# TensorE's order in the gated-DeltaNet recurrence of a hybrid decoder step, written out by hand

## The chip, the core and the metric

The kernel runs on one core of a Trainium2 chip. The metric is the device time of one execution in microseconds (us); less is better. Engines are named as in the profile: PE (TensorE), PEld (its weight loads), DVE (VectorE), ACT (ScalarE), POOL (GpSimd) and SP (SyncE, which here issues most of the DMAs).

## What is computed

One inference step of a two-layer decoder for a prompt of 256 tokens and eight samples of one token each, 264 columns in all, in float32. Each sub-layer ends in a LayerNorm. Layer 0 holds half a feed-forward block, the mixer, cross-attention and a second half feed-forward; layer 1 holds a spatial gating block in the mixer's place. The change is in the mixer:

```
proj = h @ ab_w_in                                  # 1024 -> 3*512 (q,k,v) + 512 (z) + 8 + 2*512 (ga, gb)
q, k, v = split(silu(causal_conv4(qkv)))            # 4 heads of 128
q, k = l2_normalize(q) * 128**-0.5, l2_normalize(k)
beta, g = sigmoid(b), -exp(A_log) * softplus(a + dt)
o, S = gated_delta_rule(q, k, v, g, beta, S0)       # chunks: solve (I + M) sol = rhs, then a scan over chunks
o = rms_norm(o, dn_norm_g) * silu(z)
c = causal_conv31(ga * sigmoid(gb))                 # depthwise, 512 channels
c = silu(layer_norm(c + cc_conv_b))
y = concat([o, c]) @ ab_w_out
```

## The kernel before

Activations lie transposed, channels on the 128 partitions and the 264 tokens along the row. Every projection is cut into units of 128 output channels. A unit is 24 matmuls, called products here: 8 slices of the 1024 inputs, each three times, since operands are split into a high and a low part of a shorter float format (`Unit.products`, line 659; high by high, low by high, high by low). The weights come in blocks of 256 output channels (1 MB, `load_w`, line 192, tile `raw`, three buffers); for each unit ACT writes the high part (`whi`, line 224) and DVE the low part (`wlo`, line 217), four buffers of each. Products add up in one of four PSUM tiles `mm`; all small matmuls use four others, `ax`.

The mixer (`mixer`, line 828) runs in this order in the program: projections of q, k and v with their four-tap convolution (`ev_qkv`), squares for the norms (1038, 1041), gates and decay matrices DT for two chunks of 128 tokens (1061 to 1110), the inverse of a triangular matrix in five levels of blocks up to 32 (1226 to 1251), two merges of blocks to 64 and to 128, the chunk scan (1304 to 1330), and beside it a generator `sample_step` that does the eight samples' recurrence in pieces (`next(steps, None)`). Behind it stand `glu` (the gates ga and gb; gb needs a Sigmoid on ACT), `taps` (the 31-tap convolution: the gated rows are stored to DRAM, read back shifted by 0 to 3 tokens, `cinx`, and 32 small matmuls per 128 channels do four taps each, line 932), `zeta` (z), `conv_norm` (the LayerNorm behind the taps), four units of attention keys (`fill`), the output gating and `update` (new states of the samples). `attention` and `out_proj` follow.

Only some instructions are pinned to the order of the program (`pin`, line 143). For the rest a scheduler picks the order of each engine, and it pulls `glu`, `taps` and `zeta` forward between the recurrence's matmuls. `cinx` and its weights use the three `raw` buffers of the projections' weights. The lines that set this:

```
pin(PE.matmul(self.ps, lhsT=self.w[q // 2][:, k, :], rhs=self.rhs[q % 2][:, k, :], ...), pinned)      # a product
buf = wpool.tile([P, KT, 256], F32, tag="raw", name="cinx", bufs=3)                                   # the taps' input
```

Of the kernel before, what the change touches and what calls it, by code (L numbers as in the profile page):

```python
# [15 lines left out]
P = 128  # L16
# [19 lines left out]
def decoder_step_kernel(  # L36
# [235 lines left out]


    class Norm:
# [7 lines left out]
        def __init__(self, idx, scale, eps, units=None, on_pe=False, place=None):  # L282
# [5 lines left out]
            self.S = work.tile([P, T], F32, tag="lnS", name="lnS", bufs=1)  # L288
            self.Q = work.tile([P, T], F32, tag="lnQ", name="lnQ", bufs=1)
# [26 lines left out]
        def add(self, k, ps):  # L316
# [4 lines left out]
            if k == 1:  # L321
                s01 = work.tile([P, T], F32, tag="lns01", name="lns01", bufs=1)
# [8 lines left out]
                else:  # L331
                    ca = work.tile([P, T], F32, tag="lnca", name="lnca", bufs=1)
# [57 lines left out]
        def fixed(self, ps):  # L390

            w2 = work.tile([P, 2], F32, tag="fixw", name="fixw", bufs=4)
            A.copy(w2, ps[:, T:])
            t = work.tile([P, T], F32, tag="fix", name="fix", bufs=2)
            pin(V.scalar_tensor_tensor(out=t, in0=self.ndl, scalar=w2[:, 0:1], in1=ps[:, :T], op0=ALU.mult, op1=ALU.add), True)  # L395
            pin(V.tensor_tensor(out=t, in0=t, in1=self.r, op=ALU.mult), True)
            return t, w2[:, 1:2]

        def finish(self, kv, evac, at):
# [9 lines left out]
            self.ndl = work.tile([P, T], F32, tag="lnca", name="lndl", bufs=1)  # L409
# [418 lines left out]
    def mixer(nrm, fillers, mp):  # L828
# [3 lines left out]

        cp_ctx = tc.tile_pool(name="conv", bufs=1, reuse_waits="tile")
# [66 lines left out]
        gbt = {}  # L900

        def ev_gb(n, ps):
            gbt[n] = mp.tile([P, T], F32, tag="gb", name="gb", bufs=2)
            A.activation(out=gbt[n], in_=ps, func=AF.Sigmoid)
# [4 lines left out]
        def glu(n2):  # L909
            proj(ab_w_in, 2056 + 512 + 256 * n2, 2, rhs, lambda n, ps: ev_gb(2 * n2 + n, ps))  # L910
            proj(ab_w_in, 2056 + 256 * n2, 2, rhs, lambda n, ps: ev_ga(2 * n2 + n, ps))
            for n in range(2 * n2, 2 * n2 + 2):
                SP.dma_start(cin_d[n], cin[:, n, 0:30 + NP])

        def taps(n):

            W = NP + 28
            buf = wpool.tile([P, KT, 256], F32, tag="raw", name="cinx", bufs=3).rearrange("p k n -> p (k n)")
            xs = buf[:, :4 * W].rearrange("p (g t) -> p g t", g=4)
            w07 = buf[:, 4 * W:4 * W + 7 * P].rearrange("p (j g m) -> p j g m", j=7, g=4)  # L920
            w7 = mp.tile([P, 4, 32], F32, tag="cw", name="cw")
            G.memset(xs[96:128, :, W - 1:], 0.0)
            SP.dma_start(w07, cw_d[n][:, 0:7])
            SP.dma_start(w7, cw_d[n][:, 7])
            src = cin_d[n].rearrange("(g c) t -> c g t", c=32)
            for s in range(4):
                w = W - 1 if s == 3 else W
                SP.dma_start(xs[32 * s:32 * s + 32, :, :w], src[:, :, s:s + w])
            pv = mm_ps()
            for j in range(8):  # L930
                for g in range(4):
                    PE.matmul(pv[32 * g:32 * g + 32, :NP], lhsT=w07[:, j, g, :] if j < 7 else w7[:, g, :], rhs=xs[:, g, 4 * j:4 * j + NP], start=j == 0, stop=j == 7)  # L932
# [3 lines left out]
            V.tensor_scalar(out=o[:, NP:], in0=cs_[:, n, :], scalar1=par[:, n, R_CCB:R_CCB + 1], scalar2=None, op0=ALU.add)  # L936

# [59 lines left out]
        def ev_z(n, ps):  # L997
            A.activation(out=zs[:, n, :], in_=ps, func=AF.Silu)
            G.tensor_scalar(out=zs[:, n, :], in0=zs[:, n, :], scalar1=dng, scalar2=None, op0=ALU.mult)

        def zeta(h):
            proj(ab_w_in, 1536 + 256 * h, 2, rhs, lambda n, ps: ev_z(2 * h + n, ps))
# [26 lines left out]

        q, kk, v = qkv  # L1030

# [3 lines left out]
        for i, t in enumerate((kk, q)):  # L1035
            for c in range(2):
# [3 lines left out]
                for h in range(H):  # L1040
                    PE.matmul(pss[32 * h:32 * h + 32, m:m + P], lhsT=ones[1][:, 0:32], rhs=sq[:, h, :], start=True, stop=True)
        st = gp.tile([P, 512], F32, tag="Y", name="st", bufs=2)
        A.copy(st, pss)
        pss = ax_ps()
        for m in range(4):
            PE.transpose(pss[:, m * P:(m + 1) * P], st[:, m * P:(m + 1) * P], ident)
# [14 lines left out]
        PE.matmul(pc[:, 0:8], lhsT=tri, rhs=gv[:, 0:2, :], start=True, stop=True)  # L1061
# [7 lines left out]
        for c in range(2):  # L1069
            cs = TOK[c]  # L1070

            tg = gp.tile([P, H, P], F32, tag="tg", name="tg", bufs=2)
            for h in range(H):
                if 'AAAAAAAA'[4 * c + h] == 'A':
                    A.mul(tg[:, h, :], tri, gv[:, c, h:h + 1])
                else:
                    (V if 'AAAAAAAA'[4 * c + h] == 'V' else G).tensor_scalar(out=tg[:, h, :], in0=tri, scalar1=gv[:, c, h:h + 1], scalar2=None, op0=ALU.mult)
            pg = ax_ps()
            PE.matmul(pg, lhsT=ones[1], rhs=tg.rearrange("p h i -> p (h i)"), start=True, stop=True)
# [7 lines left out]
            for h in range(H):  # L1087
                A.activation(out=DT[c][:, h, :], in_=DT[c][:, h, :], func=AF.Exp, bias=ngc[:, c, h:h + 1])
            pk = ax_ps()
            for h in range(H):  # L1090
                PE.matmul(pk[:, h * P:(h + 1) * P], lhsT=kk[:, h, cs], rhs=kk[:, h, cs], start=True, stop=True)
            NT[c] = gp.tile([P, H, P], F32, tag=f"NT{c}", name="NT")
            for h in range(H):
                V.scalar_tensor_tensor(out=NT[c][:, h, :], in0=hd(pk)[:, h, :], scalar=br2[:, c, h:h + 1], in1=DT[c][:, h, :],
                                       op0=ALU.mult, op1=ALU.mult)
            pq = ax_ps()
            for h in range(H):
                PE.matmul(pq[:, h * P:(h + 1) * P], lhsT=kk[:, h, cs], rhs=q[:, h, cs], start=True, stop=True)
# [6 lines left out]

            pv = ax_ps()
            for h in range(H):
                PE.transpose(pv[:, h * P:(h + 1) * P], v[:, h, cs], ident)
# [11 lines left out]
        def sample_step():  # L1120
# [7 lines left out]
            PE.matmul(pkq[:, :64], lhsT=ones[1], rhs=kq2, start=True, stop=True)  # L1128
# [654 lines left out]
```

## Time and profile before

| what | us |
|---|---|
| three runs | 1391.05, 1386.64, 1386.5 (median 1386.64) |
| the profiled execution, its own time | 1388.67 |
| its span, first to last instruction | 1387.0 |
| PE busy | 1345.1 (97%) |
| DVE busy | 937.1 (68%) |
| ACT busy | 742.6 (54%) |
| POOL busy | 202.7 (15%) |

The table's times but the first row are of one profiled execution, and those of the engines add up what each was busy; they overlap. A busy PE is one that has matmuls under way, not one at its peak. The clock that the chip granted PE (PEclk; 1.00 is 2.4 GHz, 0.50 is 1.2 GHz) averages 0.983 over the span. The page also follows the chain of work that ended last back from the end: 71% of the span lie on PE, 44% of it on line 659, the products.

### The profile page before, as it was taken

The page shows a single profiled execution, that of the slowest core. Times are in us where ns is not written, and L with a number is a line of the kernel's source. Part 1 is how long each engine was busy: PE and PEld are TensorE (multiplying, and loading weights), DVE is VectorE, ACT ScalarE, POOL GpSimd, SP SyncE. Part 2 cuts the span into 40 slices and gives each one's busy share as a digit, 9 for nine tenths or more (in the row PEclk, how much of TensorE's full clock was granted, in tenths as well). Part 3 has the DMA queues.
Part 4 walks back from the last instruction along what each step waited for, and adds up shares of the span by engine and source line. Part 5 has one row for each costly group of instructions (what it writes and reads, how often), then busy time and mean ns, then how long its engine had stood idle before and what let it go on. Part 6 is the DMA issues. An engine that isn't in the chain of part 4 may idle for free.

```text
span 1387.0 us, 27352 instructions
## 1 busy us (share of the span) xinstructions
PE 1345.1 (97%) x10951; PEld 1272.8 (92%) x10951; DVE 937.1 (68%) x1911; ACT 742.6 (54%) x1362; POOL 202.7 (15%) x244
## 2 busy tenths in 40 slices
PE   8999999988989999999999999999999999999997
PEld 8999999866879978999999999999999868999996
DVE  5555668865658776975556865566988987855454
ACT  4455447774545544664445654445766635744432
POOL 3312410301111000111121011121112001011021
PEclk9999999999989999999999999999999999999998
DMA  7654766435659888455556655556548893555551
GB/s 261 215 165 161 240 196 178 140 110 145 185 184 313 286 276 263 149 176 182 184 177 195 215 171 181 180 175 193 186 143 275 284 304 119 188 189 183 185 175 37
DMA packets 270543, 269.27 MB, mean 194 GB/s; under 512 B 8243, under 2 KB 266291, under 8 KB 270400
## 3 DMA queue, kind: packets, MB, share of 16 engines
q1 hardware_dynamic: 257408, 260.97, 59.5%
q10 hardware_dynamic: 13008, 6.55, 1.8%
q8 instruction: 86, 1.41, 0.4%
q14 instruction: 41, 0.34, 0.1%
HBM read 252.81 MB, written 15.26 MB: 193 GB/s over the span
## 4 chain that ended last, share of the span: by engine, by line
PE 71%; DVE 5%; ACT 4%; DMA 2%; issue 1%; POOL 0%; POOLq 0%; ACTq 0%; DVEq 0%
PE mm L659 44%; PE mm L818 5%; PE mm L817 5%; PE mm L819 5%; PE mm L711 3%; PE ax L1686 1%; PE ax L1657 1%; DMA S_s<-in_state_dn_S_dram 1%; ACT whi L224 1%; PE ax L1636 1%; DVE wlo L217 1%; PE ax L1615 1%; DMA raw<-in_ab_w_in_dram 0%; PE mm L932 0%; ACT XT L1207 0%
## 5 line engine op out<-in xcount | busy, mean ns | idle before, releaser
L217 DVE TENSOR_TENSOR wlo<-raw,whi 128x1024 fp32r<-128x1024 f32 (+1 forms) x380 | 460.8, 1220 | 252.1 <-ACT whi L224 248.3
L224 ACT CAST whi<-raw 128x1024 fp32r<-128x1024 f32 (+1 forms) x380 | 389.3, 1031 | 418.9 <-PE mm L659 219.9
L659 PE MATMUL mm<-xhi,whi 128*128 128x264 f32 x1728 | 496.2, 288 | 5.3 <-ACT whi L224 5.2
L659 PE MATMUL mm<-xhi,wlo 128*128 128x264 f32 x1728 | 496.3, 288 | 3.3 <-DVE wlo L217 3.3
L659 PE MATMUL mm<-xlo,whi 128*128 128x264 f32 x1728 | 495.1, 287 | 0.2
L659 PEld LDWEIGHTS mm<-xhi,whi 128*128 128x128 f32 x1728 | 328.3, 190 | 10.2 <-ACT whi L224 6.7
L659 PEld LDWEIGHTS mm<-xhi,wlo 128*128 128x128 f32 x1728 | 327.0, 190 | 8.7 <-DVE wlo L217 4.2
L659 PEld LDWEIGHTS mm<-xlo,whi 128*128 128x128 f32 x1728 | 329.0, 190 | 2.9 <-issue 1.4
L817 PE MATMUL mm<-hh,whi 128*128 128x264 f32 x704 | 200.6, 285 | 0.0
L818 PE MATMUL mm<-hl,whi 128*128 128x264 f32 x704 | 200.1, 284 | 0.0
L819 PE MATMUL mm<-hh,wlo 128*128 128x264 f32 x704 | 199.8, 284 | 0.0
L817 PEld LDWEIGHTS mm<-hh,whi 128*128 128x128 f32 x704 | 132.6, 188 | 0.1
L819 PEld LDWEIGHTS mm<-hh,wlo 128*128 128x128 f32 x704 | 132.4, 188 | 0.0
L818 PEld LDWEIGHTS mm<-hl,whi 128*128 128x128 f32 x704 | 132.3, 188 | 0.1
L187 POOL TENSOR_TENSOR hl<-sg,hh 128x264 fp32r<-128x264 f32 x44 | 61.1, 1388 | 444.1 <-ACT hh L180 444.1
L659 PE MATMUL mm<-xpre,whi 128*128 128x266 f32 x640 | 117.3, 290 | 1.6 <-DVE fix L395 1.6
L659 PEld LDWEIGHTS mm<-xpre,whi 128*128 128x128 f32 x640 | 97.9, 189 | 2.8 <-ACT x L443 1.4
L659 PE MATMUL mm<-xpre,wlo 128*128 128x266 f32 x320 | 85.2, 288 | 0.0
L368 POOL TENSOR_TENSOR lnQ<-lnQ,lnsq 128x264 f32<-128x264 f32 x40 | 41.7, 1042 | 296.7 <-ACT lnsq L361 296.6
L765 DVE TENSOR_TENSOR sg<-mm,sg 128x264 f32<-128x264 f32 x76 | 32.9, 433 | 50.6 <-PE mm L659 50.0
L659 PEld LDWEIGHTS mm<-xpre,wlo 128*128 128x128 f32 x320 | 57.7, 189 | 0.1
L1620 DVE CUSTOM_DVE_ANT_0 junk<-cache,ax 128x256 f32<-128x256 f32 x128 | 47.3, 413 | 5.2 <-PE ax L1615 5.0
(488 smaller groups left out, 1768.1 us busy)
## 6 DMA issues: line engine op xcount, KB each, us to landing
raw<-in_ffn_w_gate_dram SPq DMA_DIRECT2D x43, 1024.0 KB, 6.3
raw<-in_ffn_w_up_dram SPq DMA_DIRECT2D x43, 1024.0 KB, 5.5
raw<-in_ffn_w_down_dram SPq DMA_DIRECT2D x32, 1024.0 KB, 5.5
cache<-in_cache_mem_k_dram SPq DMA_DIRECT2D x32, 512.0 KB, 6.3
cache<-in_cache_mem_v_dram SPq DMA_DIRECT2D x32, 512.0 KB, 7.2
raw<-in_ffn_w_down_dram SPq DMA_DIRECT2D x16, 768.0 KB, 4.5
raw<-in_ab_w_in_dram SPq DMA_DIRECT2D x12, 1024.0 KB
raw<-in_xa_wk_dram SPq DMA_DIRECT2D x8, 1024.0 KB, 5.0
```

The source lines that it names most:

```text
L187: e.tensor_tensor(out=lo, in0=src, in1=f32(hi), op=ALU.subtract)
L217: e.tensor_tensor(out=lo[:, :nk], in0=r, in1=f32(hi[:, :nk]), op=ALU.subtract)
L224: A.copy(hi[:, :nk], r)
L368: pin(e.tensor_tensor(out=Q, in0=Q, in1=sq, op=ALU.add), last)
L659: pin(PE.matmul(self.ps, lhsT=self.w[q // 2][:, k, :], rhs=self.rhs[q % 2][:, k, :], start=self.n == 1, stop=self.n == 3 * KT), pinned)
L711: pin(PE.matmul(self.ps[:, a * 256:(a + 1) * 256], lhsT=(mhi, mhi, mlo)[q][:, k, a * P:(a + 1) * P], rhs=self.w[k // 4][q % 2][:, k % 4, : ...
L765: V.tensor_tensor(out=sg, in0=pu, in1=sg, op=ALU.mult)
L817: PE.matmul(ps, lhsT=hi[:, k, :], rhs=xh, start=n == 0, stop=False)
L818: PE.matmul(ps, lhsT=hi[:, k, :], rhs=xl, start=False, stop=False)
L819: PE.matmul(ps, lhsT=lo[:, k, :], rhs=xh, start=False, stop=n == FT - 1)
L1615: PE.matmul(pq[:, b * 256:(b + 1) * 256], lhsT=sel[:, bb:bb + 1].broadcast_to([64, P]), rhs=q8n_h[h], start=True, stop=True)
L1620: V.tensor_tensor_reduce(out=junk, in0=kc[:, b, a, :], in1=pq[:, b * 256:(b + 1) * 256], scale=1.0, scalar=0.0, op0=ALU.mult, op1=ALU.add, ...
```

## The change

Every matmul and transpose of the recurrence goes through a small class `TE`, which pins it to the order of the program. A generator `stream` yields the twelve remaining units of the projections (gb, ga, z) product by product and the four sets of taps matmul by matmul, 416 items in all, and `f(n)` takes the next n of them; calls of `f` stand at each place where the chain of the recurrence waits for another engine. What is left when the chain is through comes in one piece (`f(10000)`).

Other edits that come with it:

- gb's sigmoid is a Tanh and an Identity on ACT, `0.5 * tanh(0.5 x) + 0.5`.
- The decay matrix's matmul with `ones` over the ACT result `tg` (eight multiplications) is four matmuls per chunk with the gates, broadcast, as weights and `tri` as the moving side.
- The taps' input lies in two blocks `nb0` and `nb1` that the Norm class uses for its work tiles at other times (`block`), and is read by eight DMAs of half the size, with all eight weight slices in one DMA of 512 KB.
- Levels: both chunks' first halves stand ahead of both second halves. The scaling by `dng` moves from POOL into the gating on DVE. `vb` is made by eight ACT multiplications. Two of the four `update` calls and the waits of `conv_norm` are placed by hand, the latter with products of the attention keys in them. The split of `og` is on DVE alone.

```diff
+        class TE:
+            def matmul(*a, **k):
+                pin(PE.matmul(*a, **k))
+            def transpose(*a):
+                pin(PE.transpose(*a))
...
-            A.activation(out=gbt[n], in_=ps, func=AF.Sigmoid)
+            A.activation(out=gbt[n], in_=ps, func=AF.Tanh, scale=0.5)
+            A.activation(out=gbt[n], in_=gbt[n], func=AF.Identity, scale=0.5, bias=half)
...
+        def taps_load(n):
             W = NP + 28
-            buf = wpool.tile([P, KT, 256], F32, tag="raw", name="cinx", bufs=3).rearrange("p k n -> p (k n)")
+            xs = [work.tile([P, 3 * T], F32, tag=f"nb{i}", name="cinx", bufs=1)[:, :2 * W].rearrange("p (g t) -> p g t", g=2) for i in range(2)]
+            w8 = mp.tile([P, 8, 4, 32], F32, tag="cw", name="cw")
+            SP.dma_start(w8, cw_d[n])
             src = cin_d[n].rearrange("(g c) t -> c g t", c=32)
-            for s in range(4):
-                w = W - 1 if s == 3 else W
-                SP.dma_start(xs[32 * s:32 * s + 32, :, :w], src[:, :, s:s + w])
+            for i in range(2):
+                G.memset(xs[i][96:128, :, W - 1:], 0.0)
+                for s in range(4):
+                    w = W - 1 if s == 3 else W
+                    SP.dma_start(xs[i][32 * s:32 * s + 32, :, :w], src[:, 2 * i:2 * i + 2, s:s + w])
+            return xs, w8
...
+        def stream():
+            seq = [(2056 + 512, 0, ev_gb), (2056, 0, ev_ga), 0, (2056 + 768, 2, ev_gb), 10, (2056 + 256, 2, ev_ga), 11,
+                   (1536, 0, ev_z), 12, (1536 + 256, 2, ev_z), 13]
...
+                    for _ in range(3 * KT):
+                        u.products(1, True)
+                        yield
+                    evac(n, u.ps)
+                    if evac is ev_ga:
+                        SP.dma_start(cin_d[n], cin[:, n, 0:30 + NP])
+                        if n == 0:
+                            xs[0] = taps_load(0)
+                elif q >= 10:
+                    yield from taps(q - 10, *xs[q - 10])
+                    if q < 13:
+                        xs[q - 9] = taps_load(q - 9)
...
+        f(8)
...
+            f(4 + 12 * c)
+            pg = ax_ps()
             for h in range(H):
-                if 'AAAAAAAA'[4 * c + h] == 'A':
-                    A.mul(tg[:, h, :], tri, gv[:, c, h:h + 1])
...
-            PE.matmul(pg, lhsT=ones[1], rhs=tg.rearrange("p h i -> p (h i)"), start=True, stop=True)
+                TE.matmul(pg[:, h * P:(h + 1) * P], lhsT=gv[:, c, h:h + 1].broadcast_to([P, P]), rhs=tri, start=True, stop=True)
...
+                f(8)
+            for c in range(2) if l else ():
+                px = ax_ps()
+                for b in range(4):
+                    TE.matmul(px[32 * b:32 * b + 32, :P], lhsT=xts[c][:, 32 * b:32 * b + 32], rhs=XT[c][:, b, :], start=True, stop=True)
+                V.tensor_tensor(out=XP[c], in0=XP[c], in1=px[:, :P], op=ALU.subtract)
                 spread_blocks('VVVV', X[c], XP[c])
...
+                f(8)
...
         for _ in steps:
-            pass
+            f(14)
...
-            G.tensor_tensor(out=vb[a], in0=v4.rearrange("p (o e) -> p o e", o=1).broadcast_to([P, 4, P]),
-                            in1=id8[:, 4 * a:4 * a + 4].rearrange("p (m o) -> p m o", o=1).broadcast_to([P, 4, P]), op=ALU.mult)
+            for m in range(4):
+                A.mul(vb[a][:, m, :], v4, id8[:, 4 * a + m:4 * a + m + 1])
...
-        for n in range(4):
+        f(10)
+        for n in range(2):
             update(n)
+        f(10000)
```

How the order of the engines moves, at three places. In the changed kernel line 666 is the product, 844 and 847 are the matmul and transpose of `TE`, 910 is silu, 1093 the squares, 1192 egs, 1262 the copies into X, 1306 the update of XP, 934 and 940 the loads of the taps' weights and input.

ACT at the opening, from the last piece of v's projection to the squares, before:

```order
L904 ACT_TABLE_LOAD
L904 ACTIVATE gb<-mm 128x264
L894 ACT_TABLE_LOAD
L894 ACTIVATE mixs<-mixs 128x1056
...
L904 ACTIVATE gb<-mm 128x264
L1038 ACTIVATE sq<-keys 128x512 x2
L1137 ACT_TABLE_LOAD
L1137 ACTIVATE egs<-gv 8x4
L1038 ACTIVATE sq<-mixs 128x512 x2
```

and with the change:

```order
L910 ACT_TABLE_LOAD
L910 ACTIVATE mixs<-mixs 128x1056
L1093 ACTIVATE sq<-keys 128x512 x2
L1192 ACT_TABLE_LOAD
L1192 ACTIVATE egs<-gv 8x4
L1093 ACTIVATE sq<-mixs 128x512 x2
```

`mixs` is v before its silu, then the queries; the left-out row is a third load. Both gates gb and two loads are gone from here; the gates now come later in the stream.

PE at the opening, behind the sums of the squares (`st`), before:

```order
L1046 MATMUL ax<-ident,st 128x128 x4
L1061 MATMUL ax<-gv,tri 128x8
L659 MATMUL mm<-xhi,wlo 128x264
...
L1079 MATMUL ax<-tg,ones_80 128x512
L1091 MATMUL ax<-keys 128x128 x4
L1098 MATMUL ax<-mixs,keys 128x128 x4
L1108 MATMUL ax<-ident,mixs 128x128 x4
```

and with the change:

```order
L847 MATMUL ax<-ident,st 128x128 x4
L844 MATMUL ax<-gv,tri 128x8
L666 MATMUL mm<-xlo,whi 128x264
...
L844 MATMUL ax<-tri,gv 128x128 x4
L666 MATMUL mm<-xhi,wlo 128x264
...
L844 MATMUL ax<-keys 128x128 x4
L666 MATMUL mm<-xhi,whi 128x264
...
L844 MATMUL ax<-mixs,keys 128x128 x4
L666 MATMUL mm<-xlo,whi 128x264
```

Rows left out are three more products each time. Before, the four groups of one chunk and then those of the other stand without a product between them; now four products stand ahead of each group of the first chunk, and 16, 8, 6 and 4 ahead of those of the second. In the levels it is 8 between any two groups of the chain. Ahead of the squares' first sums there were 73 products in a row, now 8.

DVE in level 1, where the update of XP is followed by the copies into X that the next matmuls wait for, with the change:

```order
L1306 TENSOR_TENSOR XP<-XP,ax 128x128
L131 SCALAR_TENSOR_TENSOR rq_y<-rq_t,rq_y 128x64
L217 TENSOR_TENSOR wlo<-raw,whi 128x1024
L1262 COPY X<-XP 32x4x32 x4
L1306 TENSOR_TENSOR XP<-XP,ax 128x128
```

A weight split now stands between the update and its copies here and at one more of the eight updates in levels 1 to 4. SP, the loads of the third set of taps:

```order
L192 DMA raw<-in_ab_w_out_dram 128x8x256
L940 DMA cinx<-cin_125 32x2x284
L934 DMA cw<-cw_129 128x1024
L940 DMA cinx<-cin_125 32x2x284 x2
L940 DMA cinx<-cin_125 32x2x283
```

The other half of the loads follows in the same way. A block of the output projection's weights stands ahead of this set, which before had none ahead of it.

## Rows read from the trace of the kernel before

**Rows 1.** The page's first part: busy time, share of the span, instructions of each engine.

```profile
PE 1345.1 (97%) x10951; PEld 1272.8 (92%) x10951; DVE 937.1 (68%) x1911; ACT 742.6 (54%) x1362; POOL 202.7 (15%) x244
```

**Rows 2.** Busy time by window (us, busy of each engine, PEclk, DMA share, GB/s).

```profile
275.50:305.20 29.70, 24.43 (x198) 20.89 (x198) 18.90 (x68) 25.32 (x50) 4.41 (x9) 0.96 0.38 115
305.20:331.10 25.90, 23.36 (x278) 15.67 (x282) 21.01 (x79) 14.51 (x46) 2.43 (x3) 0.92 0.32 94
331.10:353.20 22.10, 19.26 (x313) 15.18 (x301) 4.21 (x22) 8.95 (x25) 2.36 (x4) 0.85 1.02 244
353.20:365.50 12.30, 12.30 (x115) 10.24 (x114) 8.31 (x27) 8.73 (x33) 0.97 (x1) 1.00 0.01 3
365.50:409.50 44.00, 37.91 (x303) 30.71 (x303) 26.21 (x84) 20.33 (x51) 8.30 (x9) 0.88 0.67 208
```

**Rows 3.** Timeline of PE (start us, us; in brackets idle before and its releaser).

```profile
303.33 0.59 PE L659 MATMUL mm<-xhi,whi 128*128 128x264 f32 x1 [1.61 <-ACT whi L224]
```

**Rows 4.** Windows of PE alone (us, PE busy, PEclk, DMA share, GB/s).

```profile
304.00:306.00 2.00, 0.89 (x11) 0.50 0.00 0
```

**Rows 5.** Waits of PE, 275.5 to 409.5 (us in total, times, longest).

```profile
PE ax L1163 <- DMA S_s<-in_state_dn_S_dram: 2.5, 2, 1.5
```

**Rows 6.** Timeline of PE, two products one after the other.

```profile
310.75 0.28 PE L659 MATMUL mm<-xhi,whi 128*128 128x264 f32 x1
310.87 0.28 PE L659 MATMUL mm<-xlo,whi 128*128 128x264 f32 x1
```

**Rows 7.** Windows of PE, line 659 (products) first, then line 932 (taps).

```profile
305.20:331.10 25.90, 11.06 (x68) 0.92 0.32 94
331.10:353.20 22.10, 7.65 (x42) 0.85 1.02 244
365.50:409.50 44.00, 20.53 (x144) 0.88 0.67 208
...
305.20:331.10 25.90, 5.54 (x66) 0.92 0.32 94
331.10:353.20 22.10, 4.10 (x62) 0.85 1.02 244
365.50:409.50 44.00, 5.59 (x94) 0.88 0.67 208
```

**Rows 8.** Timeline of ACT in the opening.

```profile
279.98 1.28 ACT L894 ACT_TABLE_LOAD   x1
281.27 1.08 ACT L894 ACTIVATE mixs<-mixs 128x1056 f32<-128x1056 f32 x1
...
283.94 1.14 ACT L1038 ACTIVATE sq<-keys 128x512 f32<-128x512 f32 x2
```

**Rows 9.** Timeline of DVE in the opening.

```profile
276.97 1.91 DVE L878 SCALAR_TENSOR_TENSOR mixs<-qkvraw,par,mixs 128x256 f32<-128x256 f32 x4
```

**Rows 10.** Timeline of PE, the last square matmuls.

```profile
288.46 0.43 PE L1041 MATMUL ax<-sq,ones 128*32 128x128 f32 x8
```

**Rows 11.** Groups of instructions, 275 to 410 (xcount, busy us, mean ns, idle before).

```profile
L217 DVE TENSOR_TENSOR wlo<-raw,whi 128x1024 fp32r<-128x1024 f32 x15 | 19.1, 1292 | 4.8 <-ACT whi L224 4.8
...
L1207 DVE COPY X<-XP 32x128 f32<-32x128 f32 x40 | 9.0, 226 | 0.5
...
L1075 ACT ACTIVATE tg<-tri,gv 128x128 f32<-128x128 f32 x8 | 2.5, 391 | 0.0
...
L1166 ACT COPY sT<-ax 128x512 f32<-128x512 f32 x2 | 1.2, 588 | 4.6 <-PE ax L1163 4.6
```

**Rows 12.** DMA issues, 270 to 412 (xcount, KB each, us to landing), and line 928.

```profile
raw<-in_ab_w_out_dram SPq DMA_DIRECT2D x3, 1024.0 KB, 6.3
...
cin<-cin SPq DMA_DIRECT2D x4, 143.0 KB, 2.1
cinx<-cin SPq DMA_DIRECT2D x4, 141.5 KB, 7.6
...
L928 SPq DMA_DIRECT2D cinx<-cin x16: 302/424/477, 285.6 to 343.1; - x16
```

More of the change, by code (lines that the diff above doesn't have):

```diff
@@ L271, in ffn_units, with block @@
         return make, AF.Silu
+    def block(name, i):
+        t = work.tile([P, 3, T], F32, tag=f"nb{i}", name=name, bufs=1)
+        return [t[:, j, :] for j in range(3)]
     class Norm:
@@ L1060, in mixer @@
         pc = ax_ps()
[L1061 removed]
+        TE.matmul(pc[:, 0:8], lhsT=tri, rhs=gv[:, 0:2, :], start=True, stop=True)
         ngc = gp.tile([P, 2, H], F32, name="ngc")
@@ L1127, in sample_step @@
             pkq = ax_ps()
-            PE.matmul(pkq[:, :64], lhsT=ones[1], rhs=kq2, start=True, stop=True)
+            TE.matmul(pkq[:, :64], lhsT=ones[1], rhs=kq2, start=True, stop=True)
             V.tensor_scalar(out=kq2, in0=pkq[:, :64], scalar1=1e-6, scalar2=None, op0=ALU.add)
@@ L1148, in sample_step @@
             pqk = ax_ps()
-            PE.matmul(pqk[:, :32], lhsT=ones[1], rhs=pr.rearrange("p b h -> p (b h)"), start=True, stop=True)
+            TE.matmul(pqk[:, :32], lhsT=ones[1], rhs=pr.rearrange("p b h -> p (b h)"), start=True, stop=True)
             qk4 = gp.tile([P, NS, H], F32, name="qk4")
@@ L1433, in mixer, with conv_norm @@
             update(n)
+        f(10000)
+        def conv_norm(kf):
+            pm = mm_ps()
+            for ct in range(4):
+                PE.matmul(pm[:, :T], lhsT=ones[512], rhs=cv[:, ct, :], start=ct == 0, stop=ct == 3)
+            kf.products(28, True)
+            n = mm_ps()
+            for ct in range(4):
+                V.tensor_tensor(out=cv[:, ct, :], in0=cv[:, ct, :], in1=pm[:, :T], op=ALU.subtract)
+                sq = work.tile([P, T], F32, tag="lnsq", name="csq")
+                A.activation(out=sq, in_=cv[:, ct, :], func=AF.Square)
+                for c in range(3):
+                    pin(PE.matmul(n[:, c:c + 1], lhsT=sq[:, TOK[c]], rhs=ones[1][:, 0:1], start=ct + c == 0, stop=ct + c == 5), ct + c == 0)
+            kf.products(32, True)
+            m2 = work.tile([P, 3], F32, tag="lnm2", name="cm2")
+            V.tensor_scalar(out=m2, in0=n[:, 0:3], scalar1=1.0 / 512, scalar2=LN_EPS, op0=ALU.mult, op1=ALU.add)
+            y = rsqrt(m2, 3)
+            rs = spread(y[:, 0:1], y[:, 1:2], y[:, 2:3], True, ps=mm_ps())
+            for ct in range(4):
+                V.tensor_tensor(out=cv[:, ct, :], in0=cv[:, ct, :], in1=rs, op=ALU.mult)
+                A.activation(out=cv[:, ct, :], in_=cv[:, ct, :], func=AF.Silu, scale=par[:, ct, R_CCG:R_CCG + 1],
+                             bias=par[:, ct, R_CCBB:R_CCBB + 1])
+            kf.products(1000, True)
@@ new lines, in mixer @@
+        keys = kv_units(0, 4)
+        conv_norm(Filler(keys))
+        for n in range(2, 4):
+            update(n)
+        for u in keys:
+            u.place = mm_ps
+            u.finish()
+        for ct in range(4):
+            split_rhs(out_hi[:, 4 + ct, :], out_lo[:, 4 + ct, :], cv[:, ct, :])
+        for c in range(2):
+            pt = ax_ps()
+            for h in range(H):
+                PE.transpose(pt[:, h * P:(h + 1) * P], o_nat[c][:, h, :], ident)
+            og = gp.tile([P, H, P], F32, tag=f"DX{c}", name="og")
+            V.scalar_tensor_tensor(out=og, in0=hd(pt), scalar=dng, in1=zs[:, :, TOK[c]], op0=ALU.mult, op1=ALU.mult)
+            split_rhs(out_hi[:, 0:4, TOK[c]], out_lo[:, 0:4, TOK[c]], og, V)
```

186 lines of the change are left out of this document (81 added, 105 removed).

## The prediction

> **What bounds the kernel now.** I read the page's table of busy time first: TensorE (PE) works in 97% of the span, VectorE (DVE) in 68%, ScalarE (ACT) in 54% [rows 1]. An average like that hides stages, so next I cut the mixer, where the change lies, into five stretches with the view of busy time by window [rows 2]: the opening (squares of the keys and queries, gates, decay matrices), the levels of the triangular inverse, the merge with the sample step, the two chunks, and the tail up to the output projection's first matmul. Their lengths add up to 134.0 us. PE is idle for 5.3, 2.5, 2.8, 0 and 6.1 us of them, 16.7 in all. The column of the granted clock shows a second loss: 0.96, 0.92, 0.85, 1.00, 0.88. A stage of length L at a mean clock c held 2(1-c)L at half speed (1.2 GHz instead of 2.4), so work there took up to (1-c)L longer: 1.2 + 2.1 + 3.3 + 0 + 5.3 = 11.9 us. The clock falls where PE has stood still: a product waited 1.61 us for its split weights at 303.33 [rows 3], and the next 2-us window has the clock at 0.50 [rows 4]. The list of waits has two more of 2.5 us together for the sample states' transfer [rows 5]. So the mixer's loss is idle time and what the clock takes after it, and not the number of matmuls: products start 0.12 us apart when nothing is missing [rows 6].
>
> **What changes on PE.** No product, tap or attention filler is added or removed; they are dealt out anew. Before, the mm products of the levels, merge and tail number 68, 42 and 144 and the tap rows 66, 62 and 94, two rows to one tap, so 33, 31 and 47 taps [rows 7]. Now the program asks for fixed numbers of items (a product or a tap): 82 ahead of the first level, 128 in levels 1 to 4, 52 in the merge, 32 in the chunks; 122 and the 96 key products are left for the tail. An item costs 0.12 us. I walk the stages.
>
> *Opening, 29.7 us.* ACT is the busy engine here (25.32 of 29.70 us [rows 2]). Between v's convolution and the last square it runs a Sigmoid load and gb, a Silu load (1.28 us), silu (1.08), another Sigmoid load and gb, the squares of the keys (1.14), an Exp load and the squares of the queries [rows 8]. Now both gates come later, as Tanh, and one load stands ahead of silu. v's convolution ends on DVE at 276.97 + 1.91 = 278.88 [rows 9]; from there load 1.28 (at worst), silu 1.08, squares 1.14, Exp load 1.28, squares 1.14 end at about 284.8, against 288.46 for the last square matmul before [rows 10]: 3.7 us earlier, or 4.9 if the load runs before the convolution is over; I take 4.0. Later in the opening the second group of four tg multiplications (4 x 0.39 = 1.6, overlapping to 1.3 [rows 11]) and a third load (1.28) leave ACT: 2.5 us. Against this, PE has only 8 products pinned ahead of the squares; v's are done when DVE starts on them at 276.97 [rows 9], so it stands still for some 7 us, where it was busy before; a stretch at half clock like the one at 304, which cost the opening and the levels 1.2 + 2.1 us, must follow: -3. The second chunk's decay now waits behind 16 pinned products in a row, 1.9 us, most of it seen: -1.5. Together **+2.0**; bounds -3 (half clock for twice as long, nothing gained later) and +5.
>
> *The Trainium skill, page "ScalarE: Activation LUTs", section "What ACT_TABLE_LOAD costs", puts 1.38 us of drain on top of a load's 1.28, so an estimate by it would add 3 x 1.38 = 4.1 us to this gain. In the trace silu starts 0.01 us after its load's end [rows 8], so I do not add it.*
>
> *Levels, 25.9 us.* Idle and clock give back 2.5 + 2.1; 27 items more (128 against 68 + 33) cost 3.2: 24.5 us. The pinned order leaves 16 items, 1.9 us, between the two chunks' update and their next use. DVE needs for it a subtraction and four copies (0.23 each [rows 11]); in two of the eight half-levels the order now has a 1.29-us weight split [rows 11] between the two, some 0.5 us more than the cover has: up to 1.0 us, part of which is already among the idle time. **+1.0**; bounds -6 and +2.
>
> *Merge, 22.1 us.* Idle and clock give back 2.8 + 3.3; 21 items fewer (52 against 73) save 2.5; the copies of the sample sums, 0.59 each [rows 11], and a rest of the wait for the states (2.5 us at most, 0 at least [rows 5]; I take 1.0, since they are asked for earlier) put 2.2 back: 15.7. **+6.4**; bounds +3 and +8.
>
> *Chunks, 12.3 us.* PE was never idle. 32 pinned items are 3.8 us, some 9 more than before, and the copy of the state now stands behind products on PE as well as ahead of four squares on ACT: about 0.9. **-2.0**; bounds -3 and 0.
>
> *Tail, 44.0 us.* Idle and clock give back 6.1 + 5.3; 27 items more (218 against 144 + 47) cost 3.2. New waits: vb moves from POOL to eight ACT multiplications, priced as the tg ones at 0.39, 3.1 us, with ten taps (1.2 us) ahead: 1.9 at most, I take 1.5; the last tap load (below) 0.7; the split of og is all on DVE: about 1. Sum 44.0 - 11.4 + 3.2 + 3.2 = 39.0. **+5.0**; bounds -5 and +8.
>
> *Tap loads.* Each set of taps is now loaded by eight transfers of 71 KB and one for its weights, into one pair of blocks that the taps before have to leave. Nine issues on SP's queue at 0.42 us are 3.8; a landing has a row with 2.1 us (the gate's own store of 143 KB) and one with 7.6 (142 KB for the taps) [rows 12]. I take 2.3, nearer the lower row, because the halves are half as large: 6.1 us. The cover, 48 products and what the chain puts between them, is some 9, 15 and 5.8 us for the second, third and fourth load: 0.7 late once.
>
> *The Trainium skill, page "DMA: Bandwidth & Descriptors", section "Bandwidth", asks to batch transfers to 1 MiB or more and gives 0.95 us for one of 64 KB, which speaks against cutting four loads into eight; one after the other the eight would take an estimated 7.6 us, the landing then as in the slow row, with the loads 2 to 6 us late. The trace has no 71-KB load, so it decides nothing yet.*
>
> *The rest at nothing.* POOL's four scalings by the norm's gain go into an operation that DVE does anyway; POOL is busy in 15% of the span [rows 1]. The norm's work tiles share blocks; outside the mixer the engines' orders are the same but for this. Covered by the same products as now; the price if not is one wait per norm, below 1 us.
>
> Sum: 2.0 + 1.0 + 6.4 - 2.0 + 5.0 = **12.4 us faster**. The profiled execution took 1388.67 us (span 1387.0), 2.0 above the median of 1386.64. I take the gain off the median: **1374 us**. Its own range, with not all bounds at once, is a gain of 6 to 19: 1367 to 1381.
>
> **Rivals.** *The whole loss goes.* If stream items fill every wait and the opening's gap leaves the clock alone, idle and clock, 16.7 + 11.9, less what is counted twice where PE was idle at half clock, say 25 us: 1362. Against it: the opening's new gap.
>
> *The chain, not PE, sets the pace.* If each half-level shows a full split of 1.29 us on DVE (8 x 1.29, less the 1 us taken, 9.3), the gain shrinks to 3: about 1383, no change. For it: DVE is busy for 21.0 of the levels' 25.9 us [rows 2]. Against: only two splits stand in that place.
>
> *Slower: the one pair of tap blocks.* Before, a load could go ahead into one of three buffers; now it starts only after the taps before, and on SP's queue weight loads of 1 MB (6.3 us [rows 12]) stand ahead of it. With 3.8 + 6.3 + 7.6 = 17.7 us per load the three loads are 8.4 + 2.7 + 11.9 = 23.0 us late, PE stands behind its pinned taps, and two of the gaps are followed by half clock, some 2.7 us each by the stretch at 304. Less the 0.7 counted and the gain: 23.0 + 5.4 - 0.7 - 12.4 = +15 us, 1402. It decides once a load takes about 12 us (3 + 0 + 6.2, and the clock). Against it: the first cover is in the levels, where the DMA engines were busy for a third of the time.
>
> *Nothing changes* because the scheduler had this order already: excluded by the order of PE, which differs from the squares on; its time would be 1387.
>
> **How the numbers follow.** A measurement of this kernel tells about 0.5% (6.9 us) from no change, so faster means below 1379.7, slower above 1393.6. Forecast 0.55, whole loss 0.13, chain 0.20, tap blocks 0.12. The forecast's lowest gains lie within 0.5%, which gives 0.67 faster, 0.21 the same, 0.12 slower. The range 1361 to 1387 takes in all but the slower case and the ends of the others.
>
> **What would show it.** Right: the squares' last matmul about 4 us earlier after a gap on PE of some 7 us with a clock of 0.50 behind it; levels of about 6.1 us each; no wait of taps for their blocks above 1 us; the first matmul of the output projection some 12 us earlier. Wrong: PE waiting on cinx transfers, on the copies X in every level, or on vb for over 2 us; a clock below 0.9 over the whole of levels and tail; a difference outside the mixer.

## The result, and the profile after

The change made the kernel slower: 1398.18 us (median of four runs, 1397.18 to 1400.7) against 1386.57 us (four runs), a ratio of 1.008 with a 95% interval of 1.0064 to 1.0097. Forecast were 1374 us, with a range of 1361 to 1387. Medians and ratios, here and below, leave out one run: of ten of e4_fill56, one took 1628.57 us at a granted clock of 0.75. The profiled execution took 1397.18 us with a span of 1395.4 us, 8.4 more than the span before. The table of busy time does not tell the two kernels apart; it answers to [rows 1]:

```profile
PE 1346.7 (97%) x10963; PEld 1277.2 (92%) x10963; DVE 939.1 (67%) x1913; ACT 738.1 (53%) x1361; POOL 191.9 (14%) x241
```

The stages do. This is the view of busy time by window of the changed kernel, cut at the same instructions as [rows 2] (PE's last transposes ahead of the squares, first level, sample sums, chunks, tail), with the first 14 us of the output projection behind them:

```profile
273.60:301.70 28.10, 21.06 (x180) 19.26 (x181) 18.32 (x62) 17.75 (x38) 4.42 (x8) 0.82 0.48 150
301.70:329.30 27.60, 25.62 (x300) 18.35 (x300) 20.45 (x82) 16.08 (x49) 1.03 (x3) 1.00 0.50 149
329.30:350.20 20.90, 15.94 (x285) 12.12 (x285) 8.02 (x27) 9.44 (x28) 2.00 (x4) 0.95 0.77 218
350.20:365.40 15.20, 14.90 (x108) 14.50 (x106) 7.48 (x26) 7.80 (x28) 0.00 (x0) 0.85 0.01 4
365.40:411.90 46.50, 41.36 (x351) 32.95 (x349) 23.48 (x78) 23.02 (x59) 2.15 (x6) 0.93 0.52 154
411.90:425.50 13.60, 10.07 (x59) 9.89 (x60) 8.16 (x14) 3.82 (x5) 0.00 (x0) 0.75 0.69 220
```

The first window of the output projection in the kernel before, to compare with the last line:

```profile
409.50:423.00 13.50, 13.19 (x104) 12.64 (x104) 11.39 (x17) 6.83 (x10) 0.00 (x0) 1.00 0.99 319
```

PE's idle time in the six windows is 7.0 + 2.0 + 5.0 + 0.3 + 5.1 + 3.5 = 22.9 us, where it was 16.7 + 0.3 = 17.0 before. The clock's part, (1 - c) x L as in the prediction, is 5.1 + 0 + 1.0 + 2.3 + 3.3 + 3.4 = 15.1, where it was 11.9 + 0. In the five stages of the change alone, idle time went from 16.7 to 19.4 and the clock's part from 11.9 to 11.7, and the output projection, which had lost next to nothing, now loses 6.9. So neither loss that the change was to lessen went down by more than 0.2 us. (1 - c) x L also counts half clock under which PE stood still; weighted by PE's busy share in windows of 1 us, an estimate of ours, the clock took some 9 us before and 12 now.

Set against the forecast (the first matmul of each stage in the timeline gives the borders; both kernels' profiled executions):

| stage | forecast, us | measured, us |
|---|---|---|
| ahead of the opening (last transpose ahead of the squares at 275.42, now 273.55) | 0 | -1.9 |
| opening, from there to the first level's matmul (305.25, now 301.69) | -2.0 | -1.7 |
| levels (25.8, now 27.6) | -1.0 | +1.8 |
| merge (22.1, now 20.9) | -6.4 | -1.2 |
| chunks (12.1, now 15.1) | +2.0 | +3.0 |
| tail to the output projection's first matmul (44.2, now 46.5) | -5.0 | +2.3 |
| output projection's first block (the rest of the span's +8.4) | 0 | +6.1 |

The first row is scatter and no gain of the change: the gates' small matmul, some 15 us ahead of the opening, starts at 260.42 in the kernel before and at 258.62 in the changed one, but in e3_no_load, which has the changed kernel's program up to there, at 260.08.

Where PE waited says which queues did it. These are the five longest waits of PE from 270 to 420, changed kernel (us in total, times, longest):

```profile
PE ax L844 <- ACT sq L1093: 6.7, 2, 5.3
PE mm L666 <- DVE kvn L697: 3.5, 1, 3.5
PE ax L844 <- ACT Y L1343: 3.4, 1, 3.4
PE mm L844 <- DMA cinx<-cin: 3.2, 2, 1.8
PE ax L847 <- ACT sT L1221: 1.4, 2, 0.7
```

The first line is the gap that the forecast knew of. The other three, 10.1 us, it had at 0, 0 and 0.7. Each can be followed one queue further.

*Y.* ACT's timeline in the merge:

```profile
338.79 0.37 ACTq L1441 DMA_DIRECT2D S_s<-in_state_dn_S_dram  x1
...
341.22 0.37 ACT L1343 COPY Y<-ax 64x256 f32<-64x256 f32 x1 [1.41 <-PE ax L844]
346.31 0.98 ACT L1443 ACTIVATE S_s<-S_s,eb 128x128 f32<-128x128 f32 x3 [4.72 <-DMA S_s<-in_state_dn_S_dram]
347.32 0.38 ACT L1266 ACTIVATE XT<-ax 64x256 f32<-64x256 f32 x1
347.72 0.37 ACT L1343 COPY Y<-ax 64x256 f32<-64x256 f32 x1
```

The last copy, of the second chunk, takes 0.37 us, and its matmuls were done at 343.35, as PE's timeline shows:

```profile
342.67 0.68 PE L844 MATMUL ax<-X,NT 128*64 128x64 f32 x8
```

It stands in ACT's queue behind three multiplications of `update(0)`, which wait 4.72 us for the samples' states. The change moved the `update` calls forward in the program and pinned PE, but not ACT; the scheduler placed the multiplications there.

*kvn.* The timeline of DVE at the end of the mixer, two of its copies:

```profile
411.40 0.42 DVE L697 COPY kvn<-mm 128x256 f32<-128x256 f32 x1
...
416.56 0.42 DVE L697 COPY kvn<-mm 128x256 f32<-128x256 f32 x1 [2.30 <-DMA out_dram<-kvn]
```

and that of PE:

```profile
417.13 0.78 PE L666 MATMUL mm<-xhi,whi 128*128 128x264 f32 x2 [3.53 <-DVE kvn L697]
```

All four key units are finished in a row now, and there is one buffer `kvn`, from which the transposed keys are stored: the copy at 416.56 waits for the store of the one at 411.40, which took 4.7 us to land. The transposed keys lie in PSUM tiles `mm`, which the program asks for there (`u.place = mm_ps`), until they are copied, and the output projection gets none. In the kernel before, a copy waited for this buffer too, for 5.1 us, but PE did not wait for that copy.

*Taps.* SP's queue at the fourth load:

```profile
375.74 0.30 SPq L940 DMA_DIRECT2D cinx<-cin  x1
376.15 0.87 SPq L934 DMA_DIRECT2D cw<-cw  x1
377.07 6.54 SPq L940 DMA_DIRECT2D cinx<-cin  x7
```

and PE's timeline, the taps that use it:

```profile
383.83 0.63 PE L844 MATMUL mm<-cinx,cw 128*32 128x256 f32 x4 [1.78 <-DMA cinx<-cin]
387.45 3.65 PE L844 MATMUL mm<-cinx,cw 128*32 128x256 f32 x60 [1.47 <-DMA cinx<-cin]
```

From the first issue to the second wait's end are 11.7 us, not 6.1.

Behind the gaps the clock is at half, here by windows of PE alone (us, PE busy, PEclk, DMA share, GB/s). They lie behind the opening's gap, the wait for Y and the wait for kvn:

```profile
280.00:282.00 2.00, 1.17 (x16) 0.50 0.06 19
...
350.00:352.00 2.00, 2.00 (x11) 0.50 0.16 45
...
418.00:420.00 2.00, 2.00 (x11) 0.50 0.38 97
```

### The profile page after: what moved, and what is told of

It is laid out like the page before. It is cut to its first block, busy times and chain, and to the rows that moved or that the text cites. A ratio compares the mean times of both kernels' runs of the same rounds, so it can differ in the third digit from the quotient of the medians.

```text
span 1395.4 us, 27415 instructions
## 1 busy us (share of the span) xinstructions
PE 1346.7 (97%) x10963; PEld 1277.2 (92%) x10963; DVE 939.1 (67%) x1913; ACT 738.1 (53%) x1361; POOL 191.9 (14%) x241
## 4 chain that ended last, share of the span: by engine, by line
PE 72%; DVE 6%; ACT 3%; DMA 2%; issue 1%; POOL 0%; POOLq 0%; ACTq 0%; SPq 0%; DVEq 0%
PE mm L666 44%; PE mm L825 5%; PE mm L824 5%; PE mm L826 5%; PE mm L718 3%; PE ax L844 2%; DVE wlo L217 1%; PE ax L1752 1%; PE ax L1723 1%; PE ax L1702 1%; PE mm L844 1%; PE ax L1681 1%; ACT whi L224 1%; DMA S_s<-in_state_dn_S_dram 1%; DMA cw<-cw 0%
## 5 line engine op out<-in xcount | busy, mean ns | idle before, releaser
L373 POOL TENSOR_TENSOR lnS<-lnS,lnsq 128x264 f32<-128x264 f32 x40 | 40.6, 1014 | 295.9 <-ACT lnsq L366 295.8
```

The costliest lines, as they stand in the source:

```text
L373: pin(e.tensor_tensor(out=Q, in0=Q, in1=sq, op=ALU.add), last)
```

## The experiments

Theory A: the error of the forecast is those named waits, each from another engine's or a DMA's queue, with the clock that falls behind it. Rival B: the pinned order itself is the loss, and a wait that is taken away comes back at the next place. Every kernel ran beside the kernel before on the same chip, whose medians there were 1386.8 to 1388.0 us.

**e1_finish: the key units one by one.**

```diff
-        conv_norm(Filler(keys))
+        conv_norm(ks)                 # ks calls u.finish() 12 products after a unit's last one
...
-        for u in keys:
-            u.place = mm_ps
+        for u in ks.left:
             u.finish()
```

> The changed kernel, but each attention-key unit is transposed, copied and stored about 12 products after its last product, and not all four in a row at the end of the mixer. Reference point: the changed kernel, 1398 us. Theory A (the loss is three waits that come from other queues, each with a stretch of half clock behind it): the 3.5-us wait of the output projection's second unit for the kvn copy goes, and the half clock behind it (0.56, 0.50, 0.50 from 416 on) with it: 5 to 7 us less, about 1392. Rival B (the pinned order itself is the loss, and a wait that is removed shows up at the next place): DVE is late there anyway with og and the weight splits, 0 to 2 us less, 1396 to 1398.

Measured: 1393.6 us, ratio 1.0048 (1.0033 to 1.0063), 4.6 less than the changed kernel. There is no wait for kvn any more, and the stretch behind it runs at full clock:

```profile
412.00:414.00 2.00, 2.00 (x11) 1.00 0.36 107
414.00:416.00 2.00, 2.00 (x20) 1.00 0.94 283
```

The gain is a little under A's, far from B's. The edit does two things at once: it spreads the finishes, and without `u.place = mm_ps` the transposed keys lie in `ax` tiles and no longer in `mm`. Which of the two takes the wait away was not tried.

**e2_ymul: the samples' multiplications behind Y.**

```diff
-            A.copy(Y[up], ...)
+            y6 = A.copy(Y[up], ...).ins
...
+            with tc.issue_after(y6):
                 for i in range(8):
                     A.mul(S_s[:, i, :], ...)
```

> The changed kernel, but ACT's multiplications of the sample states by their decay are queued behind the copy Y of the last merge's second chunk (order of issue alone, no wait). Theory A: the 3.4-us wait of the merge for Y goes, and the half clock from 348 to 355 (0.50, 0.50, 0.50, 0.80) with it, 3 us: about 6 us less, 1392. Rival B: the multiplications then delay the copy of the state S or the updates' matmuls, and the wait shows up there: 0 to 2 us less.

Measured: 1392.4 us, ratio 1.004 (1.0025 to 1.0056), 5.8 less, as A says. Merge and chunks of this kernel by window (all engines):

```profile
328.90:345.80 16.90, 15.30 (x286) 11.19 (x286) 7.97 (x27) 7.76 (x22) 1.94 (x4) 1.00 0.76 215
345.80:358.30 12.50, 12.50 (x106) 12.20 (x105) 7.21 (x26) 9.29 (x33) 0.00 (x0) 1.00 0.25 77
```

The merge takes 16.9 us where the forecast had 15.7, and the chunks 12.5, at a clock of 1.00. So most of the merge's forecast gain was there (5.2 of 6.4 us), under one misplaced group of ACT's order.

**e3_no_load: without the fourth load.**

```diff
-                    if q < 13:
-                        xs[q - 9] = taps_load(q - 9)
+                    if q < 12:
+                        xs[q - 9] = taps_load(q - 9)
+                    elif q == 12:
+                        xs[3] = xs[2]
```

> The changed kernel without the fourth load of the taps' input and weights: the last 128 channels of the 31-tap convolution are computed from the third set's data. Theory A: the two waits for this load, 1.8 + 1.5 us, go and nothing else (the clock stayed at 1.00 behind them): 3 us less, 1395. The slower case of the prediction (the one pair of tap blocks is the whole loss): 10 us less or more, at or below 1388.

Measured: 1390.7 us, ratio 1.0027 (1.0013 to 1.004), 7.5 less: between the two cases. The waits for the load are gone (3.2 us). Part of the rest is clock: in the same places of the tail the changed kernel had 0.50 and 0.68 (372 to 376) and 0.50 (400 to 402), and here no window of the tail is below 1.00 until the wait for kvn:

```profile
372.00:374.00 2.00, 2.00 (x32) 1.00 0.68 219
...
390.00:392.00 2.00, 2.00 (x19) 1.00 0.19 66
```

The first of these stretches lies ahead of the load's waits, and so does the wait for Y, which is 2.0 us in this profile where the changed kernel had 3.4 (1.8 in e1_finish and 2.7 in e10_narrow, at the same order there). So 3.2 us are the load's, and the other 4.3 are not shown to be.

**e4_fill56: 56 items ahead of the squares.**

```diff
         fill_in = stream()
-        f(8)
+        f(56)
```

> The changed kernel with 56 items of the stream ahead of the first squares and not 8; 48 fewer are left for the tail. Theory A: PE's gap of 5.3 + 1.4 us at the opening is filled, the half clock from 277 to 287 goes, and the tail is 48 x 0.12 = 5.8 us shorter; gb's Tanh and two weight splits now stand ahead of the squares on ACT and cost 1 to 2 us: 6 us less, about 1392. Rival B: the chain starts later by what is filled in (3 us) and the last tap load has less to hide behind: no gain, 1396 to 1399.

Measured: 1386.2 us, ratio 0.9997 (0.9987 to 1.0007), 12.0 less, about twice A's figure. The trace shows three things that come with the edit: the first squares' wait is 2.6 instead of 5.3 us (the line below), the scheduler put Y ahead of the multiplications (its wait is gone without e2's edit), and the taps, now earlier, wait for no load. One number moves all three, since it shifts the stream against every later queue, and the gain can't be divided among them.

```profile
PE ax L844 <- ACT sq L1093: 2.6, 1, 2.6
```

**e5_all: e1, e2 and e4 together.**

> The changed kernel with three edits at once: 56 items ahead of the squares, the key units finished one by one, the samples' multiplications behind Y. Theory A (separate losses): filling the opening alone came to 1387 and had already lost the wait for Y, so only the kvn wait and its half clock are left to take: 1387 - 4.6 = 1382, and with all three effects simply added 1377. Rival B (what is removed comes back at the next place): about 1387, as with the opening alone.

Measured: 1385.9 us, ratio 0.9988 (0.9975 to 1.0). That is 0.3 less than e4_fill56 (1.2 by the ratios), where A said 4.6: nearer B. Its profiled execution has no wait for kvn, but 1.8 us for the copy kvT. Its clock in the opening (272 to 300) is 0.88 where e4's was 0.94, and behind the wait for np at 304, which both have, it fell here and not in e4_fill56, though the program is the same up to there. Windows of PE from 300 to 312, e4_fill56 and then e5_all:

```profile
300.00:312.00 12.00, 8.93 (x111) 1.00 0.41 112
...
300.00:312.00 12.00, 9.93 (x103) 0.86 0.38 109
```

By (1 - c) x L the two differences are up to 1.7 us each. So both are there: clock that was lost by chance ahead of the key units, and a wait that came back (kvT). How the missing us divide between them is open.

**e6_narrow: no row of one-column matmuls.** The norm behind the taps sums squares with twelve matmuls of one column, which the profile counts as 24 rows.

```diff
-            kf.products(28, True)
+            kf.products(16, True)
...
-                    pin(PE.matmul(n[:, c:c + 1], ...), ct + c == 0)
-            kf.products(32, True)
+                    pin(PE.matmul(n[:, c:c + 1], ...), c == 0)
+                kf.products(8, True)
+            kf.products(16, True)
```

> The kernel of e5_all, but the 12 one-column matmuls of the convolution's norm no longer stand in one row: 8 key products follow each three of them. In the changed kernel the clock fell to 0.79 and 0.50 behind that row at 398 to 403 although PE waited for nothing. Theory N (the row of narrow matmuls itself brings the clock down): no half clock there, 2 us less than e5_all. Rival: the fall has to do with waits further ahead and stays: same time as e5_all within 1 us.

Measured: 1380.9 us, ratio 0.9954 (0.9939 to 0.9969), 4.9 less than e5_all. Windows of PE behind the twelve in e5_all:

```profile
388.00:390.00 2.00, 2.00 (x12) 0.59 0.00 0
390.00:392.00 2.00, 2.00 (x12) 0.56 0.04 8
```

and the same stretch of e6_narrow:

```profile
388.00:390.00 2.00, 2.00 (x19) 1.00 0.19 66
390.00:392.00 2.00, 2.00 (x16) 1.00 0.23 66
```

Theory N holds for the clock; 1.7 us of the gain are these two windows, and the rest is not explained by it (the opening's clock was 0.94 in this profile, and it did not fall behind the wait at 304).

**e7_vbpool: vb on POOL again, in e5_all.**

```diff
-            for m in range(4):
-                A.mul(vb[a][:, m, :], v4, ...)
+            G.tensor_tensor(out=vb[a], in0=v4..., in1=id8..., op=ALU.mult)
```

> The kernel of e5_all, but vb is made by two POOL multiplications as before the change, and not by eight on ACT. If the move to ACT costs what the prediction said (1.5 us of wait, and the half clock at 370 to 373 behind it, 1.5): 2 to 3 us less than e5_all. Rival: POOL's two operations of 1.04 us come no sooner, same time as e5_all within 1 us.

Measured: 1385.3 us, ratio 0.9988 (0.9971 to 1.0005): the same as e5_all within 1 us. The move of vb cost no more than 1 us or so that POOL would not have cost (the two kernels' runs spread over 6 and 10 us).

**e8_tanh: Tanh alone, in the kernel before.**

```diff
-            A.activation(out=gbt[n], in_=ps, func=AF.Sigmoid)
+            A.activation(out=gbt[n], in_=ps, func=AF.Tanh, scale=0.5)
+            A.activation(out=gbt[n], in_=gbt[n], func=AF.Identity, scale=0.5, bias=half)
```

> The kernel before with one part of the change alone: gb by Tanh and Identity in place of Sigmoid. The prediction took the table loads that fall away on ACT's chain to the squares, 1.28 us each, as a gain: two fewer ahead of the sums is 2.5 us less than the kernel before (1384); only the order of issue around them decides whether one or two go. Rival: the loads are hidden by the other waits of the opening: within 1 us of the kernel before.

Measured: 1382.9 us, ratio 0.9962 (0.9949 to 0.9975), 5.1 less than the kernel before. The gain is clear of the noise, but the profile doesn't put it where the forecast did: from the gates' small matmul ahead of the opening (260.42 before, 258.17 here) to the first squares are 24.2 and 23.6 us, 0.6 less. From 250 to 272 the clock is 1.00 here and 0.84 in the kernel before, 3.5 us by the column, though PE's order is the same there. How much of the 5.1 is the loads stays open.

**e9_more: more items where PE still stood still.** e6_narrow with

```diff
-        f(56)
+        f(72)
...
-                f(8)
+                f(8 if l else 16)
```

> The kernel of e6_narrow with 72 items ahead of the squares (not 56) and 16 at each of the two waits of level 0 (not 8); the tail has 32 fewer. In e6_narrow PE still waited 2.6 us for the squares and 2.1 us for the first np, and the clock was 0.56 and 0.59 behind the first. Theory A (an item costs nothing where PE stands still, and a filled gap keeps the clock): 32 x 0.12 = 3.8 us, and 1.5 of half clock, less than e6_narrow's 1381: about 1376. Rival B (the chain is pushed back by what is filled in, through the gates' operations on ACT): no gain, 1380 to 1382.

Measured: 1374.3 us, ratio 0.9911 (0.9888 to 0.9935), 6.7 less than e6_narrow and faster than both kernels. The longest waits of PE from 270 to 420 in it:

```profile
PE ax L847 <- ACT sT L1221: 1.4, 2, 0.7
PE mm L1461 <- ACT mixs L950: 1.4, 1, 1.4
PE ax L844 <- ACT sq L1093: 1.1, 2, 0.8
```

And windows of PE around the squares, where the clock now stays up:

```profile
282.00:284.00 2.00, 1.86 (x16) 1.00 0.03 11
284.00:286.00 2.00, 0.96 (x20) 1.00 0.00 0
286.00:288.00 2.00, 1.91 (x26) 1.00 0.91 221
```

Little came back elsewhere: against e6_narrow's list, 1.4 us for mixs, 0.9 for a weight split and 1.0 in two more are new, where the waits for the squares, np, sT, vb and kvT are 6.6 shorter. Rival B is wrong here.

**e10_narrow: e6's edit alone, in the changed kernel.**

> The changed kernel with one edit: 8 key products behind each three one-column matmuls of the convolution's norm. Theory N (the row of twelve brings the clock down): the half clock at 398 to 403 goes, 2 us less, 1396. Rival (the clock's fall there follows from the waits for the tap load further ahead; in e3_no_load, which has the row but not those waits, the clock stayed at 1.00): the fall stays or moves, 1398.

Measured: 1396.8 us, ratio 1.0077 (1.0055 to 1.01), 1.4 less than the changed kernel and inside its spread. The clock behind the twelve is 1.00 up to 412, where in the changed kernel it was 0.79, 0.50 and 0.85 from 398 to 404, so N holds for the clock, and the waits for the load alone do not bring the fall: they are still there. That they have no part in it is not shown, since in e3_no_load the row stands without them and the clock stays up. The norm's factor, which the products used to hide, is now waited for 1.1 us, which takes back part of the gain.

**e11_two: e1 and e2 in the changed kernel.**

> The changed kernel with the key units finished one by one and the samples' multiplications behind Y; the opening as in the change. Theory A (two separate waits): 1398.2 - 4.6 - 5.8 = 1388. Rival B (what is removed comes back at the next place): not below the better of the two, 1392.

Measured: 1389.9 us, ratio 1.0017 (1.0004 to 1.0031), 8.3 less where the two alone gave 4.6 and 5.8: 2 us short of their sum, near A's 1388 and better than B's 1392.

**e12_closure: e1, e2, e3 and e10 in the changed kernel.**

> The changed kernel with all the named losses taken away but the opening's: key units finished one by one, the samples' multiplications behind Y, no fourth load (the last 128 channels of the convolution are computed from the third set's data), and no row of one-column matmuls. Theory A (the named waits are the whole error of the prediction): the prediction's 1374 comes out within some 4 us; the single results added, 1398.2 - 4.6 - 5.8 - 7.5, are 1380. Rival B (there is a loss without a name, as in the levels): above 1385.

Measured: 1381.9 us, ratio 0.9962 (0.9947 to 0.9977), 16.3 less than the changed kernel: 2 us from the sum of the single results (1380), 8 from the forecast. So the named waits are most of the error, and A's claim that they are the whole of it does not hold. The profiled execution, with a span of 1376.1 us, is at the low end of its runs (1377.5 to 1385.0); its merge is 16.9 us and its chunks are 12.6, its levels 27.6.

## Why the prediction was wrong

*The step that failed* is the merge's and the tail's "idle and clock give back" (2.8 + 3.3 and 6.1 + 5.3 us). It took the pinned order of PE for the end of PE's waiting, and did not follow the queues that PE waits for: ACT's, where the multiplications of `update` now stood ahead of Y; DVE's, with one kvn buffer for four copies in a row; and SP's. e2_ymul, e1_finish and e3_no_load take these away one at a time for 5.8, 4.6 and 7.5 us (of the last, 3.2 are the load's waits and the rest is not traced to it); e12_closure, which also spreads the row of one-column matmuls, takes them together for 16.3 of the 24 us between forecast and result. Of the other 8, the levels hold 2.8 by its profile and the merge 1.2; the rest is open. The tail's clock did not come back for two more reasons that the forecast lacked: by PE's busy share, 1.7 us each were lost behind the short waits ahead of the updates' matmuls (0.6 for rq_y and 0.7 for vb, half clock to 376) and behind that row (398 to 404). The clock's terms were also too large from the start, by what (1 - c) x L counts while PE stood still: some 9 us in place of 11.9.

*Opening*: right in sum, and in the terms that can be read one by one. The stage is 1.7 us shorter (forecast 2.0). v's convolution comes 1.8 us earlier than in [rows 9], by the scatter ahead of the opening, and the copy of the squares' sums (`st` on ACT, 288.95 before, 283.92 now) 5.0 earlier, so 3.2 by the change (forecast 4.0). PE stands still for them as forecast, and the half clock behind the gap took 2.5 us by PE's busy share (forecast 3; the 5.1 above holds 2.6 in which PE stood still anyway):

```profile
275.17 1.92 DVE L894 SCALAR_TENSOR_TENSOR mixs<-qkvraw,par,mixs 128x256 f32<-128x256 f32 x4
...
280.12 1.17 PE L844 MATMUL ax<-sq,ones 128*32 128x128 f32 x16 [5.32 <-ACT sq L1093]
```

What the forecast did not weigh is that this gap need not be there: e4_fill56 (12.0 us, with two side effects) and e9_more (6.7) fill it. That e9_more lands on 1374 is a coincidence; it is another program. *The Trainium skill, page "ScalarE: Activation LUTs", section "What ACT_TABLE_LOAD costs", adds 1.38 us of drain to a load; in e9_more a load starts at 278.44 and ends 1.28 later, and silu starts at 279.74, so that row does not show the drain, and neither does the one of the kernel before [rows 8].*

*Levels*: forecast 24.8, measured 27.6, and 27.6 again in e12_closure, so this is a loss of its own. The clock came back (1.00) and the items are as many as forecast (96 products and 32 taps); the idle time did not go: 2.0 us of 2.5 are still there. About 1 us is left that the idle time does not explain, and its cause is open. The full-split rival is not what did it: single waits were 1.0 us at most.

*Chunks*: +3.0 against +2.0; 2.3 us of it were the half clock that the wait for Y left behind, and without it (e2_ymul) the stage is 12.5 us, 0.4 more than before. So the forecast's own reasons were worth 0.4 and not 2.0, and that the number came near was luck.

*Tap loads*: mis-sized, 6.1 us against a measured 11.7, and a lateness of 0.7 against 3.2. The landing was not the 2.3 us taken from the lower row: 3.8 us lie between the last issue's end and the taps. Nor were the issues 0.42 us each: seven took 6.54 us here, where seven of the second load took 4.12 and of the third 4.39; why is open. The slower rival had the mechanism but not the size: by its covers loads of 11.7 us are 2.7 + 0 + 5.9 = 8.6 late, and measured were 3.2, since the second and third were covered. The time is near its 1402 by other causes. *The Trainium skill, page "DMA: Bandwidth & Descriptors", section "Bandwidth", with its advice to batch transfers, spoke for the longer load; the trace agrees in direction (2 to 6 us late by the estimate, 3.2 measured).*

*vb* was priced at 1.5 us of wait; the changed kernel has 0.7, and against POOL it costs nothing that can be told (e7_vbpool). *The output projection* had no term, and 6.1 us were lost there: nobody was named as waiting for the PSUM tiles that the unfinished key units hold.

## What to carry to other kernels

When one engine's order is written out, list for each wait that it keeps the instruction that ends it, and read that instruction's own queue: what stands ahead of it there, and which buffer or transfer that waits for. Work that fills a wait was worth the most here where the engine would have stood still longest, so start from the largest gap (here the opening) and move items there from the end. Place by-work in small pieces where it falls due: four finishes in a row through one buffer cost 4.6 us more than four spread out (and moved to other tiles, e1_finish).

## What the runs showed that was not expected

The clock fell behind a row of twelve one-column matmuls although PE was at work when it fell: in the changed kernel and in e1_finish, e2_ymul, e4_fill56, e5_all and e11_two it went down to 0.50 or 0.56 there; in e3_no_load and e7_vbpool, with the same row, it stayed at 1.00. In the four kernels without the row (e6_narrow, e9_more, e10_narrow, e12_closure) it stayed at 1.00. So the row makes the fall possible and not certain.

The eight profiles with the row show one difference. In the six with a fall PE had stood still for a moment shortly ahead of the row or inside it: 0.56 us for `mixs` in the changed kernel and e2_ymul, 0.81 for kvT in e1_finish and e11_two, 0.17 and 0.58 for the squares inside the row in e4_fill56 and e5_all. In e3_no_load and e7_vbpool it had not. The changed kernel:

```profile
391.67 0.71 PE L1460 MATMUL mm<-mixs,ones 128*128 128x264 f32 x2 [0.56 <-ACT mixs L950]
...
395.57 2.79 PE L1468 MATMUL mm<-ones,csq 128*128 128x1 f32 x24
```

No run tried this by itself.

The same order can run with or without a fall: the stretch from 250 to 272 had 0.84 in the kernel before and 1.00 in e8_tanh. Runs of one kernel lie 3 us or more apart (e5_all: 1383.1 to 1389.1), and the three slowest have a lower mean clock than the four fastest (0.984 against 0.986 to 0.987), so differences of 1 or 2 us between these kernels say little. What decides it stays open.
